# Attention's values projected with tokens on partitions beside the second recurrence, together with regrouped small matmuls, a changed finish and earlier weight splits

## The chip, the cores and the metric

The kernel runs on one core of one Trainium2 chip. The metric is device time in microseconds of one execution. The core has a matrix engine (TensorE, PE in the profile), three engines for elementwise work (VectorE or DVE, ScalarE or ACT, GpSimd or POOL) and SyncE (SP), which here only issues DMAs. ACT issues DMAs too. Each engine works through its own queue in a fixed order.

## The reference, cut to what matters

One decoder layer, 512 tokens of width 1024, float32. A normalised input is projected once; the columns feed an RWKV-7 time mixing and a sparse attention, whose outputs are gated, merged and projected; a gated MLP with a short convolution follows.

```python
z = rms_norm(x, norm_mix_pre) @ w_in
z_rwkv, z_nsa, z_gate = split(z)
# RWKV-7, 16 heads of 64, one state per head, token by token
sa = einsum('bhvk,bhk->bhv', state, a_t)
state = state * w_t + sa * b_t + v_t * k_t ;  y_t = state @ r_t
y = (y - mean) * rsqrt(var + GN_EPS) * ln_w + ln_b      # per head
o_a = (y + sum(r * k * r_k) * v) * g                    # bonus, then gate g
# attention, 16 query heads in 4 groups; kc,vc compressed, ks,vs selected, kw,vw window
q, kc, vc, ks, vs, kw, vw, gl = split(z_nsa)
o_b = g0 * softmax(q kc) vc + g1 * softmax(q ks) vs + g2 * softmax(q kw) vw
m = sigmoid(z_ga) * (o_a @ w_branch_rwkv) + sigmoid(z_gb) * (o_b @ w_branch_nsa)
x = x + rms_norm(m @ w_out)
x = x + rms_norm((silu(conv(h Wg)) * conv(h Wv)) @ ffn_down)
```

The change touches how vs and vw (256 columns each) are made, and the steps around the recurrence that computes y and o_a.

## The kernel before, in words

**Precision.** Each wide projection is three matmuls: operands are split into a high part and a remainder (`hh`, `hl` for the input; `split_w`, line 164, for weights). A weight block of 128 columns is loaded in two halves by SP, its high part is made by ACT (line 160, recorded as 124), the remainder by GpSimd (line 162), and `proj_steps` (line 302) then runs 24 matmuls of 128x512 in eight steps of three, and yields after each. Three buffers (`WB`) hold halves.

**Order.** Pieces of work are Python generators. `drive` (line 448) takes one step of a fill generator, the projections, after giving each spawned thread its share of steps: a thread has a delay and a rate. Program order made this way is the priority by which the library's planner lays out the engine queues from its own estimate of what is ready; `keep_in_program_order` pins an instruction behind the one before it on its engine.

**RWKV.** Heads go in two groups of four pairs. For a pair, `inputs` (line 488) projects k, r and v (each evicted by `shift`), `prep` and `couple` build the chunk matrices. For a group, `invert` (line 646) inverts 32x32 triangular blocks on VectorE, and `recur` (line 690) first completes the inverse with two times 128 matmuls of 32x32 (mt, line 705, and mm, line 728; evictions at lines 712 to 714 and 733 to 735; two copies of diagonal blocks, line 718), then walks eight chunks of 64 tokens. A chunk: xw from the state (789), `inner` and `carried` (753, 760) for y, W on VectorE, a product with TT (805), the copies UV on VectorE and ACT (809, 810), the state update (815 to 822). From chunk 3 on, `stat1` and `stat2` (lines 769 to 778) alternate: a mean on VectorE, a subtraction on GpSimd, a square on ACT, a sum of squares. `finish` (line 830) normalises a pair, transposes it (`gt`), applies ln_w and ln_b on ACT (868, 871), adds the bonus, loaded into `bvl`, on GpSimd (872), and multiplies by the gate product `pg` on VectorE (881).

**Fill around the recurrences.** Beside the first: three gate projections, k, r and v of pair 4, five more gates, the value block v0. Beside the second: two gates, two key blocks, query block q0, value blocks v1 to v3, q1 to q3 with two loads of queries between. There are four value blocks (vs and vw, two of 128 columns each), made by `plain_out` (line 476): features on partitions, tokens on the free axis, stored to DRAM. Before attention `vload` (line 998) loads them, transposes them in sixteen blocks on TensorE (`vtp`), and ACT copies them to `vt`, tokens on partitions. `vt` is used by the values products (line 1142).

**Attention and the rest.** For eight head pairs, scores (lines 1079, 1086) and values run beside further fill: q4 to q7, two key blocks, then the branch projections. The second group's finish is a thread in the first pairs. Then w_out, the MLP, and for each of four token tiles `post` (line 1359) with the final norm.

## Time and profile before

| what | value |
|---|---|
| median of 3 runs | 1169.22 us (1169.16 to 1169.35) |
| profiled execution, whole | 1171.52 us |
| its span, first to last instruction | 1169.7 us |
| mean granted TensorE clock | 0.992 |
| ACT busy / GpSimd busy | 579.5 us / 595.2 us |
| DMA | 131.95 MB, 113 GB/s on average |
| first recurrence, from mt to its last inner product | 227.0 to 282.0 us |
| second recurrence, the same | 437.3 to 488.1 us |
| last matmul of the kernel ends | 1163.1 us |

All times of single instructions are of the profiled execution, counted from the start of its span. In a timeline line the columns are start, duration, engine, source line, operation, out<-in by the program's names, shape and count; in brackets is how long the engine stood idle before it and what ended that. PE is a matmul, PEld its weight load. A matmul's duration overlaps the next one's, so on TensorE the step from start to start tells the cost. In a table of stretches, PEclk is the share of full clock that was granted.

### The profile page before, as it was taken

The numbers are of one execution on the slowest core, as the hardware profiler recorded it, in microseconds if no ns is written. First come the engines' busy times: TensorE is split into PE (matmuls) and PEld (weight loads), VectorE is DVE, ScalarE is ACT, GpSimd is POOL, SyncE is SP. The second block draws the span as 40 slices with busy tenths as digits, with TensorE's granted clock in tenths as the row PEclk, the third lists the DMA queues.
The fourth block names the chain that finished last, engine by engine and source line by source line (L and its number), as shares of the span: only waits on it lengthen the run. The fifth ranks groups of instructions, "written<-read, shape, count | busy, mean of one in ns | idle before, by whom it ended". The sixth has DMA issues, their size and how long they took to land.

```text
span 1169.7 us, 19903 instructions
## 1 busy us (share of the span) xinstructions
PE 1148.6 (98%) x7418; PEld 927.3 (79%) x7418; DVE 574.0 (49%) x1196; ACT 579.5 (50%) x1149; POOL 595.2 (51%) x537
## 2 busy tenths in 40 slices
PE   9999999999999999999999999999999999999997
PEld 7888888867878887767677778889888888888886
DVE  4236555634456563587798735754443343331103
ACT  6446663534665334477576654534444444443311
POOL 4346654335666452497666635511565556554430
PEclk9999999989999999999999999999999999999999
DMA  7522335311443662225543136641233333334421
GB/s 245 134 65 75 103 99 167 96 64 53 113 125 93 188 198 92 91 60 145 170 149 97 46 97 181 209 156 39 80 99 99 97 94 99 99 97 136 127 64 72
DMA packets 95651, 131.95 MB, mean 113 GB/s; under 512 B 34177, under 2 KB 37057, under 8 KB 95298
## 3 DMA queue, kind: packets, MB, share of 16 engines
q1 hardware_dynamic: 79634, 116.26, 33.1%
q10 hardware_dynamic: 15920, 14.42, 3.9%
q8 instruction: 58, 0.95, 0.3%
q14 instruction: 39, 0.32, 0.1%
HBM read 108.30 MB, written 19.14 MB: 109 GB/s over the span
## 4 chain that ended last, share of the span: by engine, by line
PE 87%; DVE 4%; ACT 3%; POOL 2%; issue 1%; DMA 1%; SPq 0%; DVEq 0%; ACTq 0%; POOLq 0%
PE pu L223 6%; PE pu L221 6%; PE pu L222 6%; PE dn L1317 3%; PE dn L1316 3%; PE dn L1315 3%; PE o L1142 3%; PE pt L140 3%; PE ub L1199 3%; PE ub L1201 2%; PE ub L1200 2%; PE gt L306 2%; PE gt L308 2%; PE gt L307 2%; PE v L306 2%; PE v L308 2%
## 5 line engine op out<-in xcount | busy, mean ns | idle before, releaser
L1095 ACT ACTIVATE p<-p,stt 128x384 f32<-128x384 f32 (+3 forms) x128 | 70.7, 554 | 34.5 <-DVE stt L1093 32.9
L1069 POOL TENSOR_SCALAR p<-p,stt 128x512 f32<-128x512 f32 (+1 forms) x64 | 72.3, 1139 | 25.8 <-DVE stt L1064 15.5
L1457 DVE SCALAR_TENSOR_TENSOR u<-pu,cvec,u 128x511 f32<-128x511 f32 x44 | 33.0, 750 | 101.2 <-ACT u L1456 101.2
L1093 DVE CUSTOM_DVE_ANT_0 p<-s,rh 128x384 f32<-128x384 f32 (+3 forms) x128 | 59.0, 484 | 22.7 <-PE s L1079 18.3
L1463 DVE TENSOR_TENSOR al<-u,ah 128x512 fp32r<-128x512 f32 x22 | 23.8, 1080 | 45.4 <-ACT ah L1462 45.4
L140 PE MATMUL pt<-ident,p 128*128 128x128 f32 x320 | 44.3, 272 | 0.0
L1086 PE MATMUL s<-kst,qs 128*128 128x512 f32 (+1 forms) x128 | 39.2, 396 | 4.4 <-DVE stt L1093 4.1
L1461 POOL TENSOR_TENSOR u<-u,u 128x512 f32<-128x512 f32 x22 | 28.3, 1288 | 27.3 <-DVE u L1458 26.3
L1142 PE MATMUL o<-PT,vt 128*64 128x256 f32 (+3 forms) x256 | 41.5, 443 | 0.0
L140 PEld LDWEIGHTS pt<-ident,p 128*128 128x128 f32 x320 | 37.8, 141 | 4.4 <-issue 0.4
L1069 DVE TENSOR_SCALAR p<-p,stt 128x512 f32<-128x512 f32 (+1 forms) x64 | 35.3, 580 | 0.8
L1456 ACT ACTIVATE u<-pu,cvec 128x512 f32<-128x512 f32 x44 | 33.6, 764 | 3.0 <-PE pu L1419 3.0
L1458 DVE SCALAR_TENSOR_TENSOR u<-pu,cvec,u 128x510 f32<-128x510 f32 x44 | 33.0, 749 | 1.6
L1086 PEld LDWEIGHTS s<-kst,qs 128*128 128x128 f32 x128 | 20.9, 189 | 13.5 <-DVE stt L1093 9.3
L1142 PEld LDWEIGHTS o<-PT,vt 128*64 128x64 f32 x256 | 16.6, 136 | 18.8 <-issue 16.8
L1133 ACT ACTIVATE PT<-pt 128x512 f32<-128x512 f32 x48 | 27.3, 584 | 8.0 <-PE pt L140 7.8
L1363 DVE TENSOR_TENSOR p2tm<-dn,gb 128x512 f32<-128x512 f32 x4 | 2.8, 692 | 51.2 <-ACT p2jl L1361 51.2
L1135 DVE COPY PT<-pt 128x512 f32<-128x512 f32 x32 | 21.7, 678 | 8.4 <-PE pt L140 8.3
L1462 ACT ACTIVATE ah<-u 128x512 fp32r<-128x512 f32 x22 | 13.9, 633 | 22.0 <-POOL u L1461 22.0
L1095 ACT ACTIVATION_READ_ACCUMULATOR p<-p,stt 128x1 f32 x128 | 24.2, 189 | 0.0
L664 DVE TENSOR_TENSOR XP<-XP,TM 128x30 f32<-128x30 f32 (+14 forms) x60 | 20.3, 338 | 2.0
L162 POOL TENSOR_TENSOR up3l<-up30r,up3h 128x512 fp32r<-128x512 f32 x1 | 1.3, 1295 | 38.2 <-ACT up3h L124 38.2
(1755 smaller groups left out, 3953.8 us busy)
## 6 DMA issues: line engine op xcount, KB each, us to landing
gtd<-gt ACTq DMA_DIRECT2D x16, 256.0 KB, 2.2
qs<-qd SPq DMA_DIRECT2D x32, 128.0 KB, 3.3
g<-gtd SPq DMA_DIRECT2D x16, 256.0 KB, 3.2
xt<-in_x_dram SPq DMA_DIRECT2D x4, 512.0 KB, 5.5
bvd<-bv SPq DMA_DIRECT2D x8, 256.0 KB, 2.2
bvl<-bvd SPq DMA_DIRECT2D x8, 256.0 KB, 2.9
oad<-y SPq DMA_DIRECT2D x8, 256.0 KB, 2.5
kst<-kst ACTq DMA_DIRECT2D x16, 128.0 KB, 2.5
```

The costliest lines, as they stand in the source:

```text
L140: return te.transpose(o, i, ident)
L221: te.matmul(p, wh(k), mh(k), start=first and k == 0, stop=False)
L222: te.matmul(p, wh(k), ml(k), start=False, stop=False)
L223: te.matmul(p, wl(k), mh(k), start=False, stop=last and k == n - 1)
L306: te.matmul(p, wh(k), hh[:, k, :], start=k == 0, stop=False)
L308: te.matmul(p, wl(k), hh[:, k, :], start=False, stop=k == KT - 1)
L1069: (po if b else ve).tensor_scalar(o.pe[e, b, k], o.pe[e, b, k], st[e][:, 3, i:i + 1], None, op0=OP.mult)
L1086: m = te.matmul(s_[:, :n], qt, kt[:, x, b, :n], start=x == 0, stop=x == 1)
L1093: ve.tensor_tensor_reduce(sb, parts[b], rh[e][:, (3 - qb) * 128:], -1.0, BIG, OP.add, OP.min, st[e][:, 0, i:i + 1])
L1095: sc.activation(sb, sb, AF.Exp, scale=-1.0, bias=st[e][:, 0, i:i + 1], accum_out=st[e][:, 1, i:i + 1])
L1142: te.matmul(acc[e * 64:e * 64 + 64, j * 128:], vt[:, j, b * 256 + g * 64:b * 256 + g * 64 + 64], m[e][:, c:c + n], start=False, stop=k == ...
L1199: te.matmul(p, wh(k), sh[:, k, :], start=k == 0, stop=False)
```

## The change

1. `vproj` replaces the four value blocks: for each of eight k tiles a weight tile of 128x512 (the columns of vs and vw side by side, a new input `wv`) is loaded and split, and for each of four token tiles the input is the stationary operand and the weights stream. Four accumulators (two from `pj`, two from `pz`) come out with tokens on partitions, are copied by ACT and stored; `vload` loads them straight into `vt`. It is the last piece of the fill beside the second recurrence. The first recurrence gets a sixth gate in place of v0 (NG0 from 8 to 9).
2. In `recur`, two yields stand between each half run of mt or mm (64 matmuls) and its evictions; the yields after them go from four and three to one each. The matmuls of `inner` are pinned one behind the other for chunks 0 to 6. The square leaves `stat1` and is issued after the state update of the same step.
3. In `inputs`, the splits of r's weights are issued when k's projection has done step 5, v's likewise in r's.
4. In `finish`, the bonus is loaded into `y2` (two buffers, tag TB, shared with the squares and with the gates of the first recurrence), one VectorE pass makes ln_w times the transposed y plus the bonus, and ln_b is added in the pass that multiplies by `pg`. The remainder of g2 is made by two smaller subtractions, without the copy.
5. In `post`, the sum of the two sums of squares is issued before the product.

```diff
-... NG0, NQ1, PX, FN = (30, 30), (54, 54), (67, 67), (1.05, 0.85), 8, 4, 3, 1.15
+... NG0, NQ1, PX, FN = (30, 30), (54, 54), (67, 67), (1.05, 0.85), 9, 4, 3, 1.15
...
-    def proj_steps(blk, name, p):
-        wh, wl = split_w(a["wf"][blk], name)
+    def proj_steps(blk, name, p, w=None, ahead=None):
+        wh, wl = w or split_w(a["wf"][blk], name)
...
+            if ahead is not None and k == 5:
+                ahead()
             yield
...
+        def ahead(x):
+            w[x] = split_w(a["wf"]["rkv".index(x) + 3 + 3 * p], f"{x}{p}")
...
-        yield from proj_steps(4 + 3 * p, f"k{p}", pk)
+        yield from proj_steps(4 + 3 * p, f"k{p}", pk, None, lambda: ahead("r"))
...
-        yield from proj_steps(3 + 3 * p, f"r{p}", pr)
+        yield from proj_steps(3 + 3 * p, f"r{p}", pr, w["r"], lambda: ahead("v"))
...
-        yield from proj_steps(5 + 3 * p, f"v{p}", pv)
+        yield from proj_steps(5 + 3 * p, f"v{p}", pv, w["v"])
...
+            yield
+            yield
             for h in range(2):
                 up = slice(64 * h + 32, 64 * h + 64)
...
-        for _ in range(4):
-            yield
+        yield
...
+            yield
+            yield
             for h in range(2):
                 lo = slice(64 * h, 64 * h + 32)
...
-        for _ in range(3):
-            yield
+        yield
...
-                    te.matmul(y[h][hs[(c + i) % 2], i], gr.GS[:, 1 + i, c, h, :], gr.UV[:, c, i, h, :],
-                              start=c == 0, stop=c == 0 or i >= 2)
+                    m = te.matmul(y[h][hs[(c + i) % 2], i], gr.GS[:, 1 + i, c, h, :], gr.UV[:, c, i, h, :],
+                                  start=c == 0, stop=c == 0 or i >= 2)
+                    if c < 7:
+                        tc.keep_in_program_order(m)
...
-            sq[a] = rh_.tile([128, 2 * GP, 64], F32, tag="TB", name=f"SQ{g}{a}", bufs=1)
-            sc.activation(sq[a], Y8, AF.Square)
+
+        def square(a):
+            sq[a] = rh_.tile([128, 2 * GP, 64], F32, tag="TB", name=f"SQ{g}{a}", bufs=2)
+            sc.activation(sq[a], YT[:, a].rearrange("p i h v -> p (i h) v"), AF.Square)
...
                 St = SN
+                if c >= 3 and c % 2:
+                    square((c - 3) // 2)
                 yield
             else:
                 inner(c)
+        square(2)
         stat2(2, free)
         stat1(3, free)
+        square(3)
...
-            split_to(a["g2"][p], gh, gl, f"g2{p}", 256, p=rh_, late=True, tag="TM", bufs=1)
-            po.tensor_copy(gh[64:96, 128:], gl[64:96, 128:].bitcast(F32))
+            sy.dma_start(raw, a["g2"][p])
+            tc.keep_in_program_order(sc.activation(gh, raw, AF.Copy))
+            po.tensor_tensor(gl, raw[:, :128], gh[:, :128].bitcast(F32), op=OP.subtract)
+            gx = gh[64:96, 128:]
+            po.tensor_tensor(gx, raw[64:96, 128:], gx.bitcast(F32), op=OP.subtract)
...
-            bvl = rh_.tile([128, S], F32, tag="bvl", name=f"bvl{p}", bufs=1)
-            tc.keep_in_program_order(sy.dma_start(bvl, bvd[p]))
+            y2 = rh_.tile([128, S], F32, tag="TB", name=f"y2{p}", bufs=2)
+            tc.keep_in_program_order(sy.dma_start(y2, bvd[p]))
...
-                sc.activation(y2, pt, AF.Identity, scale=lnw, bias=lnb)
+                ve.scalar_tensor_tensor(y2, pt, lnw, y2, op0=OP.mult, op1=OP.add)
...
-            po.tensor_tensor(y2, y2, bvl, op=OP.add)
...
-            ve.tensor_tensor(y2, y2, pg, op=OP.mult)
+            ve.scalar_tensor_tensor(y2, y2, lnb, pg, op0=OP.add, op1=OP.mult)
...
-            fill = itertools.chain(*gates_(3), inputs(GP, os_[GP]), *gates_(NG0 - 3, (rh_, "bvl", 1)),
-                                   plain_out(43, "v0", vd_[0], (rh_, "bvl", 1)))
+            fill = itertools.chain(*gates_(3), inputs(GP, os_[GP]), *gates_(NG0 - 3, (rh_, "TB", 2)))
...
+    def vproj():
+        acc = [pj("v0"), pj("v1"), pz("v2"), pz("v3")]
+        for k in range(KT):
+            wh = wp.tile([128, 512], F32R, tag="whi", name=f"wvh{k}", bufs=WB)
+            wl = wp.tile([128, 512], F32R, tag="wlo", name=f"wvl{k}", bufs=WB)
+            split_to(a["wv"][k], wh, wl, f"wv{k}", 512)
+            for t in range(4):
+                ts = slice(t * 128, t * 128 + 128)
+                te.matmul(acc[t], hh[:, k, ts], wh, start=k == 0, stop=False)
+                te.matmul(acc[t], hl[:, k, ts], wh, start=False, stop=False)
+                te.matmul(acc[t], hh[:, k, ts], wl, start=False, stop=k == KT - 1)
+                if k == KT - 1:
+                    z = ztile(f"v{t}z")
+                    evict(sc.activation(z, acc[t], AF.Copy))
+                    sc.dma_start(vd_[t], z)
+                yield
...
-    fr1 += [plain_out(43 + i, f"v{i}", vd_[i], zp) for i in range(1, 4)]
     drive(itertools.chain(*gates_(16 - 6 - NG0, zp), *fr1, qproj(1), *[x for i in range(2, NQ1)
-                                        for x in ((qproj(i), queries(i - 2)) if i < 4 else (qproj(i),))]),
+                                        for x in ((qproj(i), queries(i - 2)) if i < 4 else (qproj(i),))], vproj()),
           f0, *rt1)
...
-            pt = pz(f"vtp{b}")
-            for t in range(4):
-                tr(pt[:, t * 128:(t + 1) * 128], z[:, t * 128:(t + 1) * 128], ident)
-            sc.activation(vt[:, :, b * 128:(b + 1) * 128], pt.rearrange("p (t f) -> p t f", f=128), AF.Copy)
-            yield
+        for t in range(4):
+            sy.dma_start(vt[:, t], vd_[t])
+        yield
...
+        ve.tensor_tensor(ss[:, 2:3], ss[:, 0:1], ss[:, 1:2], op=OP.add)
         ve.tensor_tensor(tm, acc, gb[:, 512:], op=OP.mult)
-        ve.tensor_tensor(ss[:, 2:3], ss[:, 0:1], ss[:, 1:2], op=OP.add)
```

More of the change, by code (lines that the diff above doesn't have):

```diff
@@ L34 @@
 PR, CR, IY, FR = 0.6, 0.5, 31, 0.5
-ID, IE, RD, RR, NG0, NQ1, PX, FN = (30, 30), (54, 54), (67, 67), (1.05, 0.85), 8, 4, 3, 1.15
+ID, IE, RD, RR, NG0, NQ1, PX, FN = (30, 30), (54, 54), (67, 67), (1.05, 0.85), 9, 4, 3, 1.15
 NW, NU, PA = 13, 3, 0.25
@@ L488, in inputs @@
     def inputs(p, o):
+        w = {}
+        def ahead(x):
+            w[x] = split_w(a["wf"]["rkv".index(x) + 3 + 3 * p], f"{x}{p}")
         K = o.K = rw.tile([128, S], F32, tag="K", name=f"K{p}", bufs=2)
         pk = pj(f"k{p}")
-        yield from proj_steps(4 + 3 * p, f"k{p}", pk)
+        yield from proj_steps(4 + 3 * p, f"k{p}", pk, None, lambda: ahead("r"))
         shift(pk, K, 8 + p)
@@ L851, in finish @@
             gh = rh_.tile([128, 256], F32R, tag="gh", name=f"gh{p}", bufs=1)
-            gl = rh_.tile([128, 256], F32R, tag="gl", name=f"gl{p}", bufs=1)
-            split_to(a["g2"][p], gh, gl, f"g2{p}", 256, p=rh_, late=True, tag="TM", bufs=1)
-            po.tensor_copy(gh[64:96, 128:], gl[64:96, 128:].bitcast(F32))
+            gl = rh_.tile([128, 128], F32R, tag="gl", name=f"gl{p}", bufs=1)
+            raw = rh_.tile([128, 256], F32, tag="TM", name=f"g2{p}r", bufs=1)
+            sy.dma_start(raw, a["g2"][p])
[3 more added lines that the diff above has]
+            po.tensor_tensor(gx, raw[64:96, 128:], gx.bitcast(F32), op=OP.subtract)
             yield
-            bvl = rh_.tile([128, S], F32, tag="bvl", name=f"bvl{p}", bufs=1)
-            tc.keep_in_program_order(sy.dma_start(bvl, bvd[p]))
+            y2 = rh_.tile([128, S], F32, tag="TB", name=f"y2{p}", bufs=2)
+            tc.keep_in_program_order(sy.dma_start(y2, bvd[p]))
             yield
@@ L862, in finish @@
                 tr(pt[:, t * 128:(t + 1) * 128], Y8[:, t].rearrange("p h v -> p (h v)"), ident)
-            y2 = rh_.tile([128, S], F32, tag="TB", name=f"y2{p}", bufs=1)
             y2v = y2.rearrange("p (t s u) -> p t s u", s=2, u=64)
@@ L867, in finish @@
             if i % 2 == 0:
-                sc.activation(y2, pt, AF.Identity, scale=lnw, bias=lnb)
+                ve.scalar_tensor_tensor(y2, pt, lnw, y2, op0=OP.mult, op1=OP.add)
             else:
                 for x in range(2):
-                    sc.activation(y2v[:, :, x], ptv[:, :, 1 - x], AF.Identity, scale=lnw, bias=lnb)
-            po.tensor_tensor(y2, y2, bvl, op=OP.add)
+                    ve.scalar_tensor_tensor(y2v[:, :, x], ptv[:, :, 1 - x], lnw, y2v[:, :, x], op0=OP.mult, op1=OP.add)
             yield
@@ L878, in finish @@
             te.matmul(pg, gh[:, :128], lg1l, start=False, stop=False)
-            te.matmul(pg, gl[:, :128], lg1h, start=False, stop=False)
+            te.matmul(pg, gl, lg1h, start=False, stop=False)
             te.matmul(pg, gh[:96, 128:], lg2, start=False, stop=True)
-            ve.tensor_tensor(y2, y2, pg, op=OP.mult)
+            ve.scalar_tensor_tensor(y2, y2, lnb, pg, op0=OP.add, op1=OP.mult)
             sy.dma_start(oad[p], y2)
@@ L998, in vload @@
     def vload():
-        zs = [ztile(f"zv{b}") for b in range(4)]
-        for b in range(4):
-            sy.dma_start(zs[b], vd_[b])
+        for t in range(4):
+            sy.dma_start(vt[:, t], vd_[t])
         yield
-        for b in range(4):
-            z = zs[b]
-            pt = pz(f"vtp{b}")
-            for t in range(4):
-                tr(pt[:, t * 128:(t + 1) * 128], z[:, t * 128:(t + 1) * 128], ident)
-            sc.activation(vt[:, :, b * 128:(b + 1) * 128], pt.rearrange("p (t f) -> p t f", f=128), AF.Copy)
-            yield
         for e in range(2):
@@ L1507, in layout @@
     d = {"wf": blocks(np.concatenate(cols, axis=1))}
+    d["wv"] = np.concatenate([w_in[:, n0 + o:n0 + o + 256] for o in (1792, 2304)], axis=1).reshape(8, 128, 512)
     def halves(w):
```

## Prediction, made before the changed kernel had run

> **What bounds the kernel now.** I read the page's engine totals first, then a table of stretches cut at the stage borders, then TensorE's own waits, and last the order of single instructions where a stretch looked bad.
>
> ```profile
> PE 1148.6 (98%) x7418; PEld 927.3 (79%) x7418; DVE 574.0 (49%) x1196; ACT 579.5 (50%) x1149; POOL 595.2 (51%) x537
> ```
>
> TensorE is busy for 98% of the span and no other engine for much over half. A microsecond is won only where TensorE has less to do, stands still, or runs at a lower clock. The stretches show where the last two happen.
>
> ```profile
> core 0 of [0], span 1169.7 us
> core 0: us, PE busy (x) PEld busy (x) DVE busy (x) ACT busy (x) POOL busy (x), PEclk, DMA share, GB/s
> 227.00:249.00 22.00, 20.73 (x334) 15.74 (x335) 9.12 (x16) 12.75 (x17) 6.43 (x5) 0.77 0.16 50
> 437.00:448.00 11.00, 11.00 (x253) 9.26 (x253) 2.08 (x3) 7.00 (x8) 2.05 (x2) 0.84 0.27 89
> 448.00:488.00 40.00, 39.08 (x683) 28.86 (x677) 15.13 (x34) 11.22 (x26) 13.65 (x15) 1.00 0.30 95
> 488.00:505.00 17.00, 16.52 (x94) 13.13 (x89) 15.88 (x58) 13.33 (x41) 12.44 (x14) 1.00 0.28 94
> 505.00:575.00 70.00, 64.97 (x370) 46.73 (x369) 55.57 (x170) 49.72 (x131) 54.63 (x60) 1.00 0.38 107
> ```
>
> The first two rows are the starts of the two recurrences. TensorE reads as full there, but its granted clock is 0.77 and 0.84. Taking the lowered state as half speed, that is 22 x 0.23 x 2 = 10.1 us at half clock in the first and 11 x 0.16 x 2 = 3.5 us in the second. The last row is the early attention stage with the second group's finish in it: TensorE idles 5.0 us, and VectorE is the fullest helper (55.57 of 70). Now TensorE's waits by cause (total, times, longest):
>
> ```profile
> PE s L1086 <- DVE stt L1093: 4.1, 7, 1.3
> PE xs L815 <- ACT UV L810: 2.3, 4, 0.8
> ...
> PE s L1079 <- DVE y L881: 1.3, 1, 1.3
> ...
> PE xs L805 <- DVE TT L735: 0.9, 1, 0.9
> PE pg L880 <- POOL gh L854: 0.9, 1, 0.9
> PE r L308 <- POOL r6l L162: 0.6, 1, 0.6
> ```
>
> Apart from the first, each of these belongs to a place that the change edits.
>
> **The values, and their transposes.** Four projections of 24 matmuls go out of the fill and 8 x 4 x 3 = 96 matmuls of the same 128x512 shape come in: nothing gained there. What disappears is work at the start of attention:
>
> ```profile
> 491.70 0.60 PE L140 MATMUL vtp<-ident,zv 128*128 128x128 f32 x4
> 492.05 0.59 PE L1086 MATMUL s<-kst,qs 128*128 128x384 f32 x2
> ```
> ```profile
> L140 PE MATMUL vtp<-ident,zv x16: 270/272/329, 491.7 to 497.3; 128*128 128x128 f32 x16
> L1008 ACT ACTIVATE vt<-vtp x4: 575/582/590, 493.2 to 499.5; 128x512 f32<-128x512 f32 x4
> ```
>
> Each transpose lasts 272 ns, but they overlap: the next matmul starts 0.35 us after a group of four. Sixteen take 16 x 0.35 / 4 = 1.4 us of TensorE's line; laid end to end they would be 16 x 0.272 = 4.4 us. I take **-1.4**, because in a full engine the step between starts is what counts. [...] The four ACT copies (4 x 0.58 = 2.3 us) lie beside TensorE's fill, so I count them as nothing; if ACT held TensorE there, they would be gained too. The four stores and four loads stay, the loads straight into the final tile; the first use of that tile is the values product after the first score block, several microseconds behind the loads as before. One gate projection and v0 change places between the two recurrences, 24 matmuls for 24.
>
> The new accumulators need two banks of each of two pools, and the fourth query projection has just filled one of them. Its eviction, an ACT copy like the row above (0.58) and a VectorE pass behind it (0.69, the y L881 row below), takes 1.3 us; only three matmuls (3 x 0.23) precede the second accumulator. That is a wait of **+0.6** once, or nothing if the planner puts other work there.
>
> **The bunches.** This is the largest term.
>
> ```profile
> 227.04 3.80 PE L705 MATMUL mt<-x 32*32 32x32 f32 x128
> ```
> ```profile
> 242.88 0.63 PE L307 MATMUL gt<-hl,gt14h 128*128 128x512 f32 x1
> 243.30 0.63 PE L308 MATMUL gt<-hh,gt14l 128*128 128x512 f32 x1
> ```
> ```profile
> 445.74 0.39 PE L307 MATMUL q<-hl,q2h 128*128 128x512 f32 x1
> 445.96 0.40 PE L308 MATMUL q<-hh,q2l 128*128 128x512 f32 x1
> 446.29 2.21 PE L728 MATMUL mm<-TT,x 32*32 32x32 f32 x128
> ```
> ```profile
> 232.89 4.06 ACT L718 ACTIVATE TT<-XL 32x1024 f32<-32x1024 f32 x2
> ```
>
> A run of 128 tiny matmuls (3.80 us) is followed by half clock: wide matmuls then start 0.42 us apart instead of 0.23. The run of 2.21 us at 446.29, with wide matmuls on both sides, leaves the clock at 1.00 from 448 on. The change cuts each run in two and puts two fill steps, six wide matmuls or 1.4 us, after each half (1.9 us for mt). Both halves then look like the harmless run. It also moves ACT's evictions and the 4.06 us of copies two steps back, so that the next projection's weight split gets an ACT slot before them; today TensorE starves behind those copies (the TT wait of 0.9, and 22.00 - 20.73 = 1.3 idle in all). Half clock costs 1 - 0.23/0.42 = 45% of 13.6 us, 6.1 us, if every instant were wide matmuls; about 2.5 us of it is the tail of the run, narrow matmuls and the starved wait, so 5.0. With the idle 1.3 the ceiling is 6.3. I take four fifths, 5.0, since one of the three episodes may stay. Against it, each further change between narrow and wide work costs some 0.1 us each way (445.96 to 446.29 is 0.33 instead of 0.23): four more interruptions, +0.8. Net **-4.2**; the ends are +0.8 and -5.5.
>
> The pins on the inner products only keep sixteen matmuls together. No row prices them; I take zero, between ends of 0.3 us either way that I estimate as three changes of 0.1.
>
> Three more yields before the chunks lengthen the second recurrence: at 0.85 per fill step it ends 3.5 steps later, while the fill still ends at step 90. What covers the tail is the fill of the next stage, hoisted:
>
> ```profile
> L306 PE MATMUL q<-hh,q4h x6: 393/500/504, 476.4 to 486.9; 128*128 128x512 f32 x6
> ```
>
> Six of eight steps of q4 already run there, so this supply works. If it failed for 3.5 steps, 3.5 x 3 x 0.23 = 2.4 us would be exposed; I take a quarter, **+0.6**.
>
> **The squares.**
>
> ```profile
> 261.34 0.63 ACT L775 ACTIVATE SQ<-YT 128x512 f32<-128x512 f32 x1 [3.95 <-POOL YT L773]
> 261.88 0.36 ACT L810 ACTIVATE UV<-xs 64x256 f32<-64x256 f32 x1
> ```
>
> ACT stands 3.95 us for a square that needs GpSimd's subtraction, and the UV copy, on the recurrence's own chain, waits behind it. TensorE's row for that wait says 2.3 us. The change issues the square after the UV copy and the state update. What is queued behind the square now is the next chunk's UV copy, a chunk away. **-2.3**; ends -0.5 (one of four goes) and -2.9, the row plus the 0.6 of a copy.
>
> **Weight splits ahead.** The r and v weights are split while the projection before still has two steps to go. The row for r is 0.6, so **-0.6**, between 0 and twice that (v alike). The queue past which the loads move is SP's; they are the same loads, one step earlier.
>
> **The finish.** Per pair, ACT's affine pass and GpSimd's sum go, and VectorE does both in one pass over PSUM:
>
> ```profile
> L872 POOL TENSOR_TENSOR y<-y,bvl x8: 1269/1290/1742, 307.0 to 568.0; 128x512 f32<-128x512 f32 x8
> L881 DVE TENSOR_TENSOR y<-y,pg x8: 647/686/689, 308.5 to 572.9; 128x512 f32<-128x512 f32 x8
> ...
> L868 ACT ACTIVATE y<-gt,vec x4: 763/778/779, 306.1 to 550.2; 128x512 f32<-128x512 f32 x4
> ```
>
> GpSimd loses 1.29 and ACT 0.78 a pair; VectorE gains about the 0.69 of its similar pass, four times in the 505-575 stretch: 2.8 us, to 58.4 of 70. The wait of 1.3 for y goes, because nothing waits for GpSimd's sum any more. Half of the 0.9 for gh may go, as one subtraction on a quarter of the rows replaces a copy behind the full one; I count none. The fuller VectorE returns some: +0.4, a tenth of the 4.1 that TensorE waits for it. **-0.9**; ends -1.8 and +1.5 (all 2.8 on the path, less 1.3).
>
> **The end.** After the last matmul:
>
> ```profile
> 1163.94 0.69 DVE p2tm L1363
> 1164.63 0.08 DVE p2ss L1364
> ...
> 1164.73 0.30 ACT p2r L124
> ```
>
> The sum of squares now precedes the product, so the root (0.30) runs beside the product (0.69): **-0.3**, or 0 if the planner had its own order.
>
> **Sum**: -1.4 + 0.6 - 4.2 + 0.6 - 2.3 - 0.6 - 0.9 - 0.3 = -8.5 us, against the profiled span of 1169.7 us. The profiled execution took 1171.52 in all, 2.3 more than the median of 1169.22; I carry the difference over to the median: **1160.7 us**.
>
> **Rivals.** *The clock falls all the same* (chance 0.20). [...] Then 5.0 of the bunch term stays away: 1165.7. For it: the first recurrence is also lowered after two short runs of mm, where TensorE starved. Against it: the 2.21 us run. [...]
>
> *VectorE becomes the bound* (0.10) between 505 and 575: finish at its bad end of +1.5 instead of -0.9, 1163.1. For it: TensorE's longest wait is already on VectorE. Against: ACT and GpSimd release it earlier.
>
> *Slower: the SP queue is held* (0.08). The bonus is now loaded into a buffer that the squares, the gates and the y of two pairs earlier share, and the load keeps its place in SP's queue; every weight load queues behind it.
>
> ```profile
> SPq L857 <- POOL y L872: 26.7, 5, 8.9
> ```
>
> Today such loads hold the queue for 26.7 us in five waits, the longest 8.9. Weights in hand last two half projections, 24 matmuls or 5.5 us, so a wait of 8.9 would leave 3.4 us; in five places +17, 1177.7. It cancels the gain at 1.7 us each and makes the kernel measurably slower from 2.2. Against it: two buffers now replace one, and GpSimd's sum, which released it, is gone.
>
> **How the numbers follow.** The forecast has 0.62. About 0.2%, 2.3 us, is what a measurement can tell, so faster means below 1166.9 and slower above 1171.6. Faster: 0.62 + 0.09 of VectorE's 0.10 + 0.15 of the clock's 0.20 = 0.86. Same: 0.05 of the clock's (with the tail uncovered, 1165.7 + 1.8 = 1167.5), 0.01 of VectorE's and 0.02 of SP's, 0.08. Slower: the rest of SP's, 0.06. The lower end adds the best ends: bunches -1.3, waits +0.6 and +0.6 gone, r -0.6, transposes -3.0, together -7.1 of which I allow 6.2: 1154.5. The upper end is the clock rival with 1.3 us of uncovered tail: 1167.0.
>
> **What would show it.** Granted clock 1.00, or close, at both starts, and no wide matmuls 0.42 apart; no square between GpSimd and UV; no TensorE wait on r, y or UV; no vtp; q4 still hoisted behind the last values. The prediction is wrong if the clock row still reads under 0.9, if TensorE idles more before the attention stage, or if SP's waits grow past 8.9 with weights late.

## The result, and the profile after

The changed kernel takes **1179.72 us** (median of 4 runs, 1178.71 to 1180.97) against 1169.28 us (4 runs, 1169.16 to 1170.03) for the kernel before beside it: ratio **1.0086, 95% interval 1.007 to 1.0102**, 10.1 us slower by that ratio. The forecast was 1160.7 us, range 1154.5 to 1167.0. The sign is wrong.

The profiled execution has a span of 1176.9 us, 7.2 longer than before. First the engine totals, then the same stretches as before the change.

```profile
PE 1148.9 (98%) x7402; PEld 926.2 (79%) x7402; DVE 586.0 (50%) x1208; ACT 573.4 (49%) x1133; POOL 583.2 (50%) x529
```
```profile
core 0: us, PE busy (x) PEld busy (x) DVE busy (x) ACT busy (x) POOL busy (x), PEclk, DMA share, GB/s
227.00:249.00 22.00, 19.53 (x329) 14.73 (x329) 9.74 (x16) 13.30 (x18) 5.49 (x4) 0.92 0.18 59
437.00:448.00 11.00, 11.00 (x155) 8.97 (x154) 1.16 (x2) 2.91 (x5) 2.56 (x2) 0.92 0.25 66
448.00:488.00 40.00, 38.06 (x691) 28.84 (x690) 11.99 (x28) 15.97 (x28) 13.41 (x14) 1.00 0.20 63
488.00:505.00 17.00, 15.08 (x147) 11.37 (x148) 11.69 (x34) 9.18 (x24) 7.72 (x10) 1.00 0.38 125
505.00:575.00 70.00, 66.39 (x353) 46.71 (x352) 58.39 (x183) 45.61 (x127) 50.87 (x57) 0.98 0.34 100
```

TensorE is as busy as before (1148.9 against 1148.6) over a longer span: what was added is idle time. The granted clock of the two starts did rise, from 0.77 to 0.92 and from 0.84 to 0.92. The loss stands in TensorE's waits. These rows are the largest of those that are new or grew:

```profile
PE xs L828 <- ACT UV L823: 3.5, 5, 0.9
PE v L1008 <- DVE q3zl L996: 2.5, 1, 2.5
PE g L614 <- DVE AR L579: 2.5, 6, 1.0
...
PE gt L306 <- ACT gt14h L124: 2.0, 1, 2.0
PE y L769 <- ACT UV L823: 2.0, 2, 1.3
```

The rows of r, of pg for gh and of y L881 are gone, and so are the transposes vtp. The row for UV, which the change of the squares should have emptied, grew from 2.3 in four waits to 3.5 in five, with 2.0 more before the inner products.

Where along the kernel the time went can be read from single products that both traces hold. The table gives how much longer (+) each stretch between two such starts was than in the kernel before, in us. The stretches begin where the first product of projection k0 starts, because the stretch before it (53.7 us) came out 0.3 us shorter to 2.3 longer in the profiled executions, though its code is the same in all kernels here. The profiled execution of the kernel before took 1171.52 us, 2.2 more than its median, and that of the changed kernel 1.0 less than its own, so the sum for the changed kernel can lie some 3 us under the timed difference.

| stretch (times in the kernel before) | changed kernel | without pins | squares bound |
|---|---|---|---|
| k0 (53.7) to first mt (227.0) | +0.8 | +0.7 | +0.8 |
| first recurrence: first mt to k5 (286.9) | +0.8 | -0.6 | -2.2 |
| k5 to second mt (437.3) | +2.7 | +0.7 | +2.9 |
| second mt to first score block (488.1) | +2.7 | -0.3 | -0.2 |
| score block to q5 (531.0) | +2.6 | +0.4 | +0.9 |
| q5 to the first output block (600.8) | -2.0 | -3.2 | -2.8 |
| from there to the last matmul | -0.1 | +0.1 | +0.1 |
| sum | +7.5 | -2.2 | -0.5 |

The last two columns are experiments told below.

### The profile page after: what moved, and what is told of

It reads as the page before. It is cut to its first block, busy times and chain, and to the rows that moved or that the text cites. A ratio compares the mean times of both kernels' runs of the same rounds, so it can differ in the third digit from the quotient of the medians.

```text
span 1176.9 us, 19851 instructions
## 1 busy us (share of the span) xinstructions
PE 1148.9 (98%) x7402; PEld 926.2 (79%) x7402; DVE 586.0 (50%) x1208; ACT 573.4 (49%) x1133; POOL 583.2 (50%) x529
## 4 chain that ended last, share of the span: by engine, by line
PE 82%; DVE 7%; ACT 3%; issue 3%; POOL 3%; DMA 2%; SPq 0%; DVEq 0%; POOLq 0%; ACTq 0%
PE pu L221 6%; PE pu L223 6%; PE pu L222 6%; PE o L1168 3%; PE dn L1343 3%; PE dn L1342 3%; PE dn L1341 3%; PE pt L140 3%; PE ub L1225 3%; PE ub L1227 2%; PE ub L1226 2%; PE s L1112 2%; PE gt L308 2%; PE gt L306 2%; PE gt L307 2%
## 5 line engine op out<-in xcount | busy, mean ns | idle before, releaser
L1095 POOL TENSOR_SCALAR p<-p,stt 128x512 f32<-128x512 f32 (+1 forms) x64 | 72.6, 1145 | 29.6 <-DVE stt L1090 11.5
L1119 DVE CUSTOM_DVE_ANT_0 p<-s,rh 128x384 f32<-128x384 f32 (+3 forms) x128 | 59.2, 485 | 22.8 <-PE s L1105 17.1
L1168 PE MATMUL o<-PT,vt 128*64 128x256 f32 (+3 forms) x256 | 44.5, 444 | 0.0
L813 POOL TENSOR_TENSOR SD<-S,Dc 128x256 f32<-128x256 f32 x12 | 7.5, 621 | 27.4 <-DVE S L833 25.1
```

What stands on the lines that cost most here:

```text
L1095: (po if b else ve).tensor_scalar(o.pe[e, b, k], o.pe[e, b, k], st[e][:, 3, i:i + 1], None, op0=OP.mult)
L1119: ve.tensor_tensor_reduce(sb, parts[b], rh[e][:, (3 - qb) * 128:], -1.0, BIG, OP.add, OP.min, st[e][:, 0, i:i + 1])
L1168: te.matmul(acc[e * 64:e * 64 + 64, j * 128:], vt[:, j, b * 256 + g * 64:b * 256 + g * 64 + 64], m[e][:, c:c + n], start=False, stop=k == ...
```

## The experiments

My theory after the result was that the new order makes new waits; the rival, that one of the parts costs by its own work (the finish's VectorE passes above all). Eighteen kernels followed: the parts alone (the end was not, and the squares only bound to a place), the change without one or more parts, and combinations. Ratios are to the kernel before, run beside each; 0.001 is 1.17 us.

**Each part alone.** The edits are the change's own hunks, put singly into the kernel before. Values (the projection vproj, vload without transposes, NG0 = 9):

```
-    fr1 += [plain_out(43 + i, f"v{i}", vd_[i], zp) for i in range(1, 4)]
+   ... queries(i - 2)) if i < 4 else (qproj(i),))], vproj()),
```

> The kernel before with the values alone changed: v projected with tokens on partitions at the end of the second recurrence's fill, no transposes, one gate projection in v0's old place; bunches, squares, finish, weight splits as before. Theory (new waits): the bank wait of the second accumulator behind the VectorE half of the last query eviction (2.5 us in the profile of the changed kernel) with the drop of the clock that follows it (about 1.5), and less fill left for the first score blocks: slower by 4 to 8 us, 1173 to 1177. Rival (the values are free, the loss lies in the finish or in the bunches): between -1.4 and +0.6, 1168 to 1170.

Measured 1.0031 (1.0021 to 1.0041), +3.6 us, just short of the theory's 4 to 8 and far from the rival. Its waits have the same 2.5 us of v for q3zl as the changed kernel; the transposes' 1.4 us show nowhere: from k0 on its profiled execution is 1.2 us longer than that of the kernel before.

Bunches:

```
-        for _ in range(4):
-            yield
+        yield        (and two yields behind each half of mt and of mm)
```

> The kernel before with the halves of the mt and mm runs alone moved apart by yields. Theory (new waits): the drops after the mt runs go, but TensorE starves once behind the 4 us of copies on ACT and one drop follows that gap: a gain of 0 to 2 us, 1167 to 1169. Rival (the prediction's term): -4.2, 1165. A second rival (extra interruptions cost more than the clock gives): +1 or more.

Measured 1.0006 (0.9996 to 1.0016): no difference that can be told. The clock rose in this profile as predicted, and TensorE's idle time took part of it back:

```profile
227.00:249.00 22.00, 19.52 (x322) 14.98 (x320) 9.95 (x16) 14.49 (x19) 5.48 (x4) 0.92 0.17 58
437.00:448.00 11.00, 11.00 (x217) 8.94 (x216) 1.79 (x3) 4.99 (x6) 1.41 (x2) 1.00 0.29 93
```
```profile
235.79 1.20 PE L729 MATMUL mm<-TT,x 32*32 32x32 f32 x64
...
240.29 0.50 PE L306 MATMUL gt<-hh,gt14h 128*128 128x512 f32 x1 [2.03 <-ACT gt14h L124]
```

```profile
234.94 4.01 ACT L720 ACTIVATE TT<-XL 32x1024 f32<-32x1024 f32 x2
238.98 0.60 ACT L473 ACTIVATE gt<-gt 128x512 f32<-128x512 f32 x1
239.60 0.63 ACT L124 ACTIVATE gt14h<-gt140r 128x512 fp32r<-128x512 f32 x1
```

The first fence has the two starts: 0.92 and 1.00 for 0.77 and 0.84. In the second TensorE stands 2.03 us for the gate's weights, and the third says why: on ACT their split still comes behind the 4 us of copies, now with the eviction of the gate before between them. Idle time in the first stretch goes from 1.3 to 2.5 us (22.00 - 19.52), and behind the gap wide matmuls start 0.42 us apart (242.31 to 242.73 us). The rest was lost later: from k0 on the kernel is 1.5 us ahead at the first score block and level again at q5, and the granted clock reads 0.98 from 505 to 575 us, where it was 1.00.

In eight kernels the granted clock at the starts is mostly higher where the runs are cut, though not always. With whole runs the first start (227 to 249 us) reads 0.77 in the kernel before, with the values alone and with the finish alone, and 0.84 with the bound squares alone; the second (437 to 448 us) reads 0.84, 0.84, 1.00 and 1.00. With cut runs the first reads 0.92 with the bunches alone, in the changed kernel and without its pins, and 0.77 with the squares bound in it; the second reads 1.00, 0.92, 1.00 and 1.00. The first row is from a kernel with cut runs that comes below (the changed kernel with the squares bound), the second from the next one, where the runs are whole:

```profile
227.00:249.00 22.00, 20.00 (x298) 14.90 (x300) 9.20 (x14) 13.34 (x17) 4.99 (x4) 0.77 0.16 50
437.00:448.00 11.00, 11.00 (x260) 9.34 (x255) 2.35 (x4) 7.38 (x8) 1.77 (x2) 1.00 0.25 82
```

Finish (one VectorE pass over PSUM with the bonus, lnb in the pass with the gate; with it the bonus loaded into y2 and the smaller remainder of g2):

```
-                sc.activation(y2, pt, AF.Identity, scale=lnw, bias=lnb)
-            po.tensor_tensor(y2, y2, bvl, op=OP.add)
+                ve.scalar_tensor_tensor(y2, pt, lnw, y2, op0=OP.mult, op1=OP.add)
```

> The kernel before with the finish alone changed: lnw and the bonus in one VectorE pass over PSUM, lnb in the pass with the gate, the bonus loaded into y2 itself. Theory: VectorE has the room, and the wait for y goes: 0 to -1.5 us, 1168 to 1169. Rival (VectorE or the held SP queue costs in the early attention stage): +1.5 to +6, 1171 to 1175.

Measured **0.997** (0.9958 to 0.9983), -3.5 us, better than the theory. TensorE's busy time in the 70 us of the early attention stage rises from 64.97 to 67.33 us while VectorE's goes from 55.57 to 59.94:

```profile
505.00:575.00 70.00, 67.33 (x388) 48.81 (x387) 59.94 (x180) 47.37 (x129) 52.26 (x57) 1.00 0.42 125
```

So the rival that the finish costs by its work fell here. Weight splits ahead:

```
+            if ahead is not None and k == 5:
+                ahead()
```

> The kernel before with the weight splits of r and v alone moved two steps ahead. The parts tried so far add to about +1 (values +3.6, bunches +0.7, finish -3.5), so some 9 us of the change's 10.4 are in this part or in the parts together. Theory 1 (this part): the r and v split subtractions stand ahead of couple's work in the helpers' queues and move it, and the g and AR waits of the changed kernel (2.5 us) come from it: +1 to +4, 1172 to 1175. Theory 2 (the loss is only in the parts together): -0.6 to +1, 1170 to 1172.

Measured 1.0017 (1.0006 to 1.0028), +2.0 us: theory 1, in its lower half.

```profile
PE g L614 <- DVE AR L579: 1.9, 6, 0.4
...
PE r L308 <- POOL r6l L162: 0.6, 1, 0.6
```

The wait for r that it was to remove is still there, and couple's products wait for AR 1.9 us where they waited 0.3. From k0 on the profiled execution is 0.7 us shorter than that of the kernel before, so where the 2.0 us lie is not shown.

Pins:

```
+                    if c < 7:
+                        tc.keep_in_program_order(m)
```

> The kernel before with the inner products alone pinned in their order on TensorE. The parts alone add to +2.8 (values +3.6, bunches +0.7, finish -3.5, weight splits +2.0), the whole to +10.1, and the squares as written leave ACT's order as it was. Theory 1 (the pins carry what is missing: sixteen matmuls that need both UV copies can no longer step aside): +3 to +7, 1173 to 1177. Theory 2 (the loss is in the parts together): within 0.6 of no change, 1170 to 1171.

Measured 1.002 (1.0007 to 1.0032), +2.3 us, between the theories. Its waits for the UV copies are already those of the changed kernel:

```profile
PE xs L817 <- ACT UV L812: 3.4, 5, 0.9
...
PE y L760 <- ACT UV L812: 1.9, 2, 1.3
```

The squares as the change writes them were not run alone. What they do to ACT's order can be read from the changed kernel with and without them (next group): the same squares stand ahead of the UV copies in both. So here they were bound:

```
-            sc.activation(sq[a], Y8, AF.Square)                  (in stat1)
+            m = sc.activation(sq[a], YT[:, a]..., AF.Square)     (after the state update)
+            tc.add_manual_dep(m.ins, uva.ins.name, ...)          (uva: the UV copy of the chunk on ACT)
```

> The kernel before with the squares issued after the state update as in the change, and each bound by a dependency to stand behind the UV copy of its chunk on ACT, which the change alone did not do (the rows of the changed kernel show the square ahead of UV as before). Theory (the 2.3 us wait for UV is the square's): -1.5 to -2.5 us, 1167 to 1168. Rival (the square's delay comes back through the buffer or as another wait on the chain): -0.5 to +0.5, 1169 to 1170.

Measured 1.0019 (1.0009 to 1.0028): slower, against both. In the profile the UV wait is gone and the kernel is 7.9 us ahead at the first score block, counted from k0; by q5 it is 2.0 behind. Between them TensorE has these two waits, for the split of kwp1 and for a y of the finish, together 5.7 of the 9.9 us lost there:

```profile
PE kwp L308 <- POOL kwp1l L162: 3.0, 1, 3.0
PE s L1088 <- DVE y L890: 2.7, 1, 2.7
```
So the binding works, and its gain is lost at the start of attention.

**The change without parts.**

```
after_no_splits:          the changed kernel, proj_steps and inputs as before
after_no_values:          the changed kernel, values as before
no_values_squares_pins:   bunches, finish, weight splits and the end alone
no_squares_pins:          the same with the values
after_no_pins:            the changed kernel without keep_in_program_order(m) in inner
after_no_squares:         the changed kernel with the squares issued in stat1
```

> The changed kernel without the weight splits ahead. Theory 1 (the splits carry a good part of the loss): 3 us or more faster than the changed kernel, at most 1177. Theory 2 (the parts together): 0 to 2 us faster, 1178 to 1180.

1.0076 (1.0059 to 1.0093), theory 2: the splits carry about 1 us of the ten, which the intervals do not tell from nothing.

> The changed kernel with the values as before, transposes and all. If the values' part costs what it costs alone, 3.6 us less than the changed kernel: 1176. Theory (it eats the fill that covers the tail of the recurrence and the first score blocks, and its bank wait and clock drop stand in the way): 5 to 9 us less than the changed kernel, 1171 to 1175. Rival (the loss is in the others): within 1.5 us of the changed kernel.

1.0041 (1.0027 to 1.0055), 5.3 us less than the changed kernel: theory, at its edge. More than 4 us stay.

> The changed kernel without the values, the squares and the pins: bunches, finish, weight splits and the end alone. Theory 1 (these parts add as they did alone, and squares and pins in this company cost 5 to 6): -1, 1169. Theory 2 (the bunches and the finish spoil each other): at least +3, 1173 or more.

0.9984 (0.9974 to 0.9993), theory 1. With squares and pins the same parts gave 1.0041, so these two cost 6.7 us here.

> The changed kernel without the squares and the pins, the values in. By theory 1: 3.6 to 5 above the run without values, 1173 to 1174, and 5 to 7 under the changed kernel. By theory 2 (squares and pins cost nothing): as the changed kernel, 1179 to 1180.

1.0014 (1.0003 to 1.0026), theory 1, but by more than it said: 8.4 us less than the changed kernel, where it had 5 to 7, and 3.5 above the run without values.

> The changed kernel without the pins on the inner products. Without squares and pins it came to 1171.1, with both to 1180. Theory 1 (the pins do it: with the sixteen products kept together TensorE reaches the next use of UV sooner, and waits for it 5 times instead of 2, with y's second half waiting 1.3 us in each recurrence): 1171 to 1173. Theory 2 (the squares as issued do it): 1178 to 1180. Theory 3 (only both together): 1171 to 1173 here and in the run without the squares.

**1.0004** (0.9993 to 1.0016).

> The changed kernel without the change of the squares, pins in. Theory 1 (pins): 1178 to 1180. Theory 2 (squares): 1171 to 1173. Theory 3 (only both together): 1171 to 1173.

**1.0086** (1.0071 to 1.0101). Both runs say theory 1: the pins cost 9.6 us, the squares as issued nothing that can be measured. What the pins change on another engine shows on ACT. These rows are the last square that has a UV copy beside it in the first recurrence and in the second, in the changed kernel:

```profile
283.82 0.63 ACT L788 ACTIVATE SQ<-YT 128x512 f32<-128x512 f32 x1 [1.78 <-POOL YT L784]
284.36 0.36 ACT L823 ACTIVATE UV<-xs 64x256 f32<-64x256 f32 x1
...
493.50 0.63 ACT L788 ACTIVATE SQ<-YT 128x512 f32<-128x512 f32 x1 [5.09 <-POOL YT L784]
494.03 0.36 ACT L823 ACTIVATE UV<-xs 64x256 f32<-64x256 f32 x1
```

And in the kernel without pins, in the second:

```profile
489.04 0.38 ACT L821 ACTIVATE UV<-xs 64x256 f32<-64x256 f32 x1 [3.03 <-PE xs L816]
490.12 0.63 ACT L786 ACTIVATE SQ<-YT 128x512 f32<-128x512 f32 x1 [0.70 <-POOL YT L782]
```

With the pins the square stands ahead of the UV copy, and ACT waits for GpSimd's subtraction while TensorE's data lie ready; without them the copy goes first. In the changed kernel all six squares that have a UV copy in their chunk stand so; without pins it is three (264.36, 284.81 and 471.33 us), in the kernel before four. TensorE's waits for the UV copies, 3.5 and 2.0 us with the pins, are these without:

```profile
PE xs L826 <- ACT UV L821: 1.5, 2, 0.8
...
PE y L769 <- ACT UV L821: 0.9, 1, 0.9
```

In the changed kernel the products that wait are the inner ones too, which the pins keep where they are:

```profile
283.04 0.45 PE L769 MATMUL y<-UV,GS 128*64 128x64 f32 x8 [0.21 <-DVE UV L822]
284.77 0.45 PE L769 MATMUL y<-UV,GS 128*64 128x64 f32 x8 [1.28 <-ACT UV L823]
```

If that is the way, binding the squares must take the pins' cost away with the pins left in. The edit is the binding shown above, put into the changed kernel.

> The changed kernel, pins in, with each square bound by a dependency to stand behind the UV copy of its chunk on ACT. Theory 1 (the pins bring y and its statistics forward, so the squares slip ahead of the UV copies, and the waits for UV, 3.5 and 2.0 us, and the clock drops behind them are the cost): the UV waits under 1 us together, 1169 to 1173. Theory 2 (the order on TensorE itself costs, whatever ACT does): 1177 to 1181. Rival 3 (time won in the second recurrence is given back at the start of attention, as with squares bound in the kernel before): UV waits gone, but 1174 to 1177.

**0.9998** (0.9986 to 1.0011): theory 1. One dependency per square is worth 10.3 us to the changed kernel. The waits of this run, from its list:

```profile
PE g L614 <- DVE AR L579: 2.6, 6, 1.0
PE v L1011 <- DVE q3zl L999: 2.5, 1, 2.5
PE gt L306 <- ACT gt14h L124: 2.0, 1, 2.0
...
PE xs L831 <- ACT UV L826: 0.4, 1, 0.4
```

UV is down from 5.5 us in all to 0.4; the others stand as they were. By the table the profiled execution is 8.0 us shorter from k0 on: 2.9 in the first recurrence, 3.0 in the second, 2.5 in attention. The waits give 5.1 of it. The clock gives nothing: it was at half in four stretches of 3.4 us after the start and before the tail in the changed kernel and for 17.1 us here (0.77 from 227 to 249 us, 0.99 from 290 to 437, 0.98 from 505 to 575). What makes up the rest was not separated.

So the pins' cost is shown, and that it goes when the squares stand behind the copies; the price of the way between is not. Of the 9.7 us by which the profiles with and without pins differ from k0 on, the waits for UV give 3.1 (5.5 against 2.4) and longer matmuls 3.4 (TensorE is busy for 1148.9 us against 1145.5, with four half-clock stretches against one, in the 0.92 from 227 to 249 us); the rest stays open. With the pins alone in the kernel before, all six squares stand ahead of the copies as well and the waits for UV are 5.3 us, but the cost is 2.3: the pins cost 9.6 only in the company of the other parts, and which of them makes it so is not shown. No kernel without pins had the squares bound together with the rest of the change, so how much of the 10.3 us is the binding's own gain is open too; in the kernel before, without any pins, it won 7.9 us up to the first score block.

**The bank wait.** The last query's remainder (q3zl) holds a bank that the values want:

```profile
430.40 2.88 DVE L692 COPY TT<-XL 32x1024 f32<-32x1024 f32 x2
433.31 0.69 DVE L996 SCALAR_TENSOR_TENSOR q3zl<-q,q3zh 128x512 fp32r<-128x512 f32 x1
```
```profile
431.13 0.39 PE L1010 MATMUL v<-wvl,hh 128*128 128x512 f32 x1
434.06 0.50 PE L1008 MATMUL v<-wvh,hh 128*128 128x512 f32 x1 [2.54 <-DVE q3zl L996]
```

It is a 0.69 us pass, queued behind VectorE's copies of the inverse.

```
-        acc = [pj("v0"), pj("v1"), pz("v2"), pz("v3")]
+        acc = [pz("v0"), pz("v1"), pj("v2"), pj("v3")]
```

> The changed kernel with the accumulators of the values taken in the other order: the two free banks of the small pool for the first two token blocks, the two of the pool that the query projections use for the last two. Nine wide matmuls instead of three stand ahead of the bank that the last query eviction holds, 1.4 us more. Theory (the bank wait of 2.5 us and the half-clock stretch behind it, 1.5): the wait falls to 1.1 or less; faster than the changed kernel by 1.4, or by 3 if the stretch goes too. Rival (time won in the second recurrence is lost at the start of attention): within 0.7 of the changed kernel.

1.0075 (1.006 to 1.009), which decides nothing: the 1.3 us less are the theory's number, but the intervals overlap, and the wait that was to fall to 1.1 is 2.55 us here too. It was not the test that it was meant to be, because in both kernels nine wide matmuls already stand ahead of the held bank. It did show something else, told at the end.

**What wins together.**

```
finish_and_pinned_squares:  the kernel before + finish + squares bound in both recurrences
finish_squares_first_only:  the same + the end, squares bound only where g == 0
best_with_values:           this + values with banks swapped
best_gate_before_values:    this with the change's banks, *gates_(16 - 6 - NG0, zp) moved from the
                            head of the fill to just ahead of vproj()
```

> The kernel before with the finish of the change and the squares bound behind the UV copy. The squares alone won 5.9 us up to the first score block and gave 10 back by 535 us, where TensorE waited 3.0 us for a weight split on GpSimd (kwp1l), 2.7 us for y and stood at half clock twice. Theory (GpSimd, full of the finish's sums there, gave the gain back): with the finish's sums off GpSimd the gain stays and the two are worth more together than apart, -6 to -10 us, 1160 to 1165. Rival (anything won ahead of the attention stage is lost there): the finish's own -3.5 at most, 1167 or more.

0.9994 (0.9984 to 1.0005): the rival. Between the first score block and q5 the kernel loses 5.6 us. GpSimd is still behind the longest wait there, but by other work than the finish's sums:

```profile
501.98 3.12 POOL L1080 TENSOR_SCALAR p<-p,stt 128x256 f32<-128x256 f32 x4
505.07 4.07 POOL L848 TENSOR_TENSOR YT<-YT,gst 128x512 f32<-128x512 f32 x4
509.10 1.26 POOL L162 TENSOR_TENSOR kwp1l<-kwp10r,kwp1h 128x512 fp32r<-128x512 f32 x1
510.32 1.27 POOL L162 TENSOR_TENSOR kwp1l<-kwp11r,kwp1h 128x512 fp32r<-128x512 f32 x1
```

From 494 us to here GpSimd works almost without a pause, mostly on the softmax weights p, then 4.07 us on the normalisation of y, and only then on the low part of kwp1's weights, for which TensorE waits 3.0 us. The finish's sums were not what stood ahead of it.

> The kernel before with the finish, the end, and the squares bound behind UV in the first recurrence only; in the second they stand as before. Squares pinned in both gained 2.2 us in the first recurrence and 2.7 in the second and lost all of it between 500 and 535 us. Theory (what is won in the second recurrence meets a helper, GpSimd, that is full at the start of attention, and what is won in the first moves everything behind it alike): the finish's -3.5 and -2.2, together -5 to -6, 1164 to 1166. Rival (any time won before attention is lost at its start): -3.5 at the most, 1167 or more.

**0.9962** (0.9947 to 0.9977), 1164.77 us: the theory's time, though -4.4 us by the ratio is short of its -5 to -6, and the interval overlaps with the finish alone (0.997). By the profiles, counted from k0, the kernel is 8.6 us shorter than the kernel before and the finish alone 4.7; the first recurrence has 3.6 of it, and that gain stays.

> The kernel before with the finish, the end, the squares pinned in the first recurrence only, and the values with their banks swapped; bunches, pins and weight splits left out. Without the values this was 1164.8. Theory (the values' part costs by its bank wait, and by fill that it takes from the first score blocks): 1164 to 1167. Rival (the transposes' 1.4 us come in once the wait is short): 1162 to 1164.

0.9958 (0.9945 to 0.9971): theory; it cannot be told from the run without the values.

> The run best_with_values with the banks in the change's order and the one gate projection of this stage moved from the head of the fill to between the last query and the values, 24 wide matmuls, 5.4 us, in which VectorE's half of the query eviction frees its bank. Theory (the values cost by the bank wait of 2.6 us and the 1.5 us of a half-clock stretch behind it): no wait of the values for a bank, 2.6 to 4 us faster than best_with_values at 0.9958, so 0.992 to 0.9936 of the kernel before. Rival (what is won there is lost again at the start of attention): 0.995 to 0.997.

**0.9948** (0.9932 to 0.9965), 1163.20 us, 6.1 us less than the kernel before: the list of TensorE's waits, which the bank wait would head, now begins so:

```profile
PE s L1111 <- DVE stt L1118: 2.1, 6, 0.6
PE warm L116 <- DVE zero L111: 1.6, 1, 1.6
PE xs L824 <- ACT UV L819: 1.5, 2, 0.8
```

The profile, counted from k0, is 4.0 us shorter than best_with_values, as the theory has it; the timed ratios overlap and their interval holds both the theory's 0.9936 and the rival's 0.995. This kernel is faster than both the kernel before and the changed one.

## Why the prediction was wrong

The step that failed is this one: "The pins on the inner products only keep sixteen matmuls together. No row prices them; I take zero, between ends of 0.3 us either way". They cost 9.6 us (1.0086 with, 1.0004 without). I bounded them by what they do on TensorE and left out what an order fixed on one engine does to the planner's order on another: all six squares stand ahead of the UV copies on ACT instead of three, and with the squares bound behind the copies the loss is gone (0.9998). How the 9.6 us add up is known only in part: 3.1 of waits for UV and 3.4 of longer matmuls. Without the pins the rest of the change is worth nothing (1.0004), not -8.5, so other terms were too hopeful as well.

- *Squares, -2.3.* The wait was rightly read as the square's, but that a later place in the program puts it behind the copy was assumed; the planner took it forward again. As issued it is worth 0 (1.0086 without it too); bound, it is worth 10.3 us in the changed kernel and costs 2.2 in the kernel before.
- *Bunches, -4.2.* In the changed kernel's profile the clock rose in both places as forecast, but the idle time of 1.3 us in the first stretch, which I had counted among the gains, became 2.5. Alone the part is worth 0 within its interval. The reading under it was too strong: whole runs are not always followed by half clock (1.00 at the second start with the finish alone), and halves not always spared (0.77 at the first start with the squares bound). The lines of half clock at 242.88 us that I showed do not even follow the run of 3.80 us: they stand behind mm, where the granted clock is 0.50 from 240.1 to 246.9 us, and the stretch of the run itself (0.50 from 229.8 to 233.2 us) begins before the run ends. So the clock's rival, that the clock falls all the same, came true at the first start with the squares bound (0.77), but not in the changed kernel (0.92 at both starts), where the stretches follow waits of 2.02 and 2.54 us.
- *Values, -1.4 + 0.6.* The transposes went, and the part costs +3.6 alone. The bank wait was named and sized at 0.6, from an idle VectorE; it was 2.5 because q3zl queues behind 2.88 us of copies.
- *Weight splits, -0.6.* +2.0 alone; couple's wait for AR grew by 1.6 us there, and the wait for r stayed. In the changed kernel the r wait is gone and the splits carry about 1, not told from nothing.
- *Finish, -0.9.* Right in sign, too small; -3.5 alone. VectorE had the room, and the wait of 1.3 for y went.
- *Tail, +0.6.* Without the pins the stretch to the first score block came out at -0.3; q4 was hoisted as before.
- *End, -0.3.* The order is as said and the root lies beside the product, but the time from the last matmul to the end went from 6.6 to 6.5 us only. Over all profiles the term holds: 6.60 to 7.04 us in the eight kernels without the end, 6.15 to 6.52 in the twelve with it. The three rows:

```profile
1171.23 0.16 DVE L1389 TENSOR_TENSOR p2ss<-p2ss 128x1 f32<-128x1 f32 x1 [3.16 <-ACT p2jl L1387]
1171.31 0.68 DVE L1390 TENSOR_TENSOR p2tm<-dn,gb 128x512 f32<-128x512 f32 x1
1171.42 0.29 ACT L124 ACTIVATE p2r<-p2ss,vec 128x1 f32<-128x1 f32 x1 [0.23 <-DVE p2ss L1389]
```

The rival on the slow side, a held SP queue, had the sign and the wrong mechanism. The load of the bonus (L878) holds the queue once, for 5.5 us, where it held it 26.7; the load of g2 (L871) reaches 11.5 us, past the mark of 8.9 that I had set, but costs nothing that shows: with the finish alone it is held for 21.5 us at the longest and the kernel is faster by 3.5, and the changed kernel's longest wait of TensorE on a weight split, 2.0 us, is for ACT's copies. In the changed kernel:

```profile
SPq L871 <- ACT gh L872: 16.1, 5, 11.5
...
SPq L878 <- DVE gst L791: 5.5, 1, 5.5
```

VectorE's rival fell with the finish's gain. One sum of the prediction is off: the best ends that it lists add up to -6.1 us, not -7.1. The range's lower end, 6.2 under the forecast, is hardly touched by it.

## What to carry to other kernels

Pinning an order on one engine is not free because its instructions stay the same: it can move what depends on them on other engines, and an instruction whose data come late can then stand in front of one that the critical path needs. Where something else plans the order, a later line in the program did not keep an instruction back here; a dependency did. The row to look at is the late instruction's neighbour on its engine. What such an order costs hung on the rest of the kernel: 2.3 us alone and 9.6 with the other parts.

Time won ahead of a stage can be lost there again. Two kernels that bound the squares in both recurrences, alone and with the finish, were 7.9 and 5.8 us ahead at the first score block and had lost it by q5. The changed kernel kept what the same binding won, and two other kernels kept what they won in the first recurrence or ahead of the second. What tells these cases apart was not shown; the longest wait in the two that lost was one for GpSimd.

## What the runs showed of the hardware

In the changed kernel the granted clock was 0.50 in four stretches between the start and the tail, each 3.4 us long, from 240.90, 285.27, 435.46 and 513.96 us. A gap of TensorE did not always lower the clock. The 2.54 us gap at 431 us in the changed kernel is followed by the stretch from 435.46 us, in which wide matmuls start 0.43 us apart. The 2.55 us gap at the same place with the banks swapped, with the same nine wide matmuls ahead of it, is not: there they start 0.23 us apart up to 436 us. What tells the two apart was not shown. Nor did a gap stand ahead of every such stretch: in the kernel before, the one from 229.81 us (0.50 up to 233.2) follows 3.4 us in which TensorE was never idle (226.4 to 229.8 us, busy for 3.40) and ran the tiny matmuls of mt from 227.04 us on.

The first 53.7 us, the same code in all kernels, differed between profiled executions: the first transposes began at 7.71 to 7.83 us in four (the kernel before, the finish alone, the pins alone, the changed kernel) and at 8.99 to 9.00 us in four others (the values, the bunches, the bound squares and the weight splits alone). In ten timed executions of the changed kernel with the squares bound the times spread over 5.7 us (1167.05 to 1172.71). Profiles of two kernels were therefore compared from a product behind the start, and small differences were left to the intervals.
